# A hybrid attention layer: row sums of full attention from ScalarE's accumulator, V's two parts in one matmul, and another split of PSUM banks in neighbourhood attention

## The chip, the cores and the metric

One Trainium2 chip, one core of it. The metric is the device time of one execution in microseconds (us); lower is better. A core has TensorE (PE in the profile; its weight loads are listed apart as PEld), VectorE (DVE), ScalarE (ACT), GpSimd (POOL) and SyncE (SP, which here issues DMAs). Each engine works through its own list of instructions in order.

## The reference

One encoder layer over 1024 tokens of width 1024, in float32, with a token grid of 16 rows and 64 columns. One input projection feeds two groups of heads:

```python
h = _rmsnorm(x, norm_gain[l]);  proj = h @ w_in[l]
q_a, k_a, v_a, g_a, q_b, k_b, v_b, g_b = jnp.split(proj, split_at, axis=-1)
# group A: 8 query heads, 2 key/value heads, head_dim 64, RMS-normed q/k, axial rope, full attention
sc = jnp.einsum('bqkgd,bskd->bkgqs', qi, k).astype(jnp.float32) * scale
p = jax.nn.softmax(sc, axis=-1)
o_a = jnp.einsum('bkgqs,bskd->bqkgd', p, v) * jax.nn.silu(g_a)
# group B: 8 heads, each query sees a clamped window of 8 rows x 16 columns, with a learned bias
o_b = _neighbourhood_attn(q_b, k_b, v_b, na_rpb[l]) * jax.nn.silu(g_b)
x = x + jnp.concatenate([o_a, o_b], axis=-1) @ w_out[l]
return _rmsnorm(x, final_norm_gain)
```

## The kernel before

Matmuls run on 16-bit operands with float32 precision kept by splitting: a float32 value is a high float16 part plus a low float16 remainder, and a product is hi*hi + hi*lo + lo*hi, so three matmuls stand where one would.

**Stages.** A head of some 85 us normalises x and makes the first weights. Then comes *stage A*, full attention: 64 steps, one for each of 2 key/value heads, 8 blocks of 128 queries and 4 query heads (`run_units(64, ...)`). Then *stage B*, neighbourhood attention: 32 steps, one for each block of 128 queries and pair of heads. Then a tail with the rest of the output projection and the final norm. Here a step of stage A or B is named by its index, from 0.

**A step of stage A.** `a_qk`: four matmuls of 512 columns give 128 x 1024 scores in the PSUM tile `s` (two such tiles take turns); DVE reads them (L732) for the row's shift `nm`; ACT takes the exponential into `p32` (L734) and copies it to the high part (L735). One step later `a_lo` on DVE makes the low part (L740), and a transposing DMA turns both into `pt`. Five steps later `a_pv` multiplies `pt` with V. V stands in `va` as 64 high columns, a column of ones, and 64 low columns. For each of 8 key blocks there are three matmuls: `pt` high by V's high part and the ones (65 columns, L757), `pt` high by V's low part (64 columns, L758), `pt` low by V's high part and the ones (65 columns, L759). Both V parts are added up in the same 64 columns of the PSUM bank `pv`, and the 65th column is the row sum. After four heads `evac` on DVE takes the reciprocal of the sums (L763), scales it (L764) and multiplies (L766).

**A step of stage B.** `b_lo` of the step before (DVE, L845), then `b_qk`: matmuls into two score banks `sb` (L815, L818); for each of two heads DVE adds the bias and takes the minimum (L836), ACT the exponential (L838); ACT copies the high part (L840). Three steps later `b_pv`. The steps of B are written so that DVE has L845, then two L836, then its other work of the step; ACT has some of its other work, then two L838 and L840, then the rest.

**Fill and jobs.** Between the attention matmuls PE is given chunks of projection matmuls (`Flow.fill`, recorded at L494): so many chunks in a step, by `FILL_A`, `FILL_B`. Their results are emptied from PSUM by *jobs* on ACT and DVE (`Flow.job`, `Flow.work`): each step has a budget for ACT and DVE, which is the step's assumed length less what attention itself takes. `BASE_A` and `BASE_B` hold these three numbers (step without fill, ACT's share, DVE's share), and what does not fit the budget waits for a later step. The jobs that prepare weights are: four sums of squares on ACT (L362), a power on POOL (L381), four high parts on ACT (L404), four low parts on DVE (L409). `need_w` issues what is still missing when a matmul asks for a weight. The first 6 steps of A are ordered by a scheduler; all later ones stand as written.

**PSUM banks in stage B.** `bank` hands out four banks, of which the scores use three in turn (`k % 3`); `proj_tile` gives the fourth to the projections, which so have three.

Of the kernel before, what the change touches and what calls it, by code (L numbers as in the profile page):

```python
# [11 lines left out]
AF = mybir.ActivationFunctionType  # L12
OP = mybir.AluOpType
AX = mybir.AxisListType
PSUM = bass.MemoryType.PSUM

P = 128
KC = 8
NU = 8
GC = 256  # L20
NH = 8
D = 64
NX = 4
BASE_A, BASE_B = (1.8, 2.6, 2.9), (1.7, 1.6, 2.0)
HAND = 6
SKEW_A, SKEW_B = 5, 3
FILL_A = [(4, 5.0), (7, 4.2)]
# [20 lines left out]
class Flow:  # L48
# [13 lines left out]
    def at(self, delay, pos, fn, *a):  # L62
        self.due.setdefault((self.slot + delay, pos), []).append((fn, a))

    def job(self, eng, cost, fn, *a, delay=1, late=1, key=None):

        self.jobs.append((late, self.slot + delay, self.number(), eng, cost, fn, a, key))
# [75 lines left out]
def kernel(ctx: ExitStack, tc: tile.TileContext, x: bass.AP, w: bass.AP, wo: bass.AP,  # L143
# [3 lines left out]
    act, dve, pool, pe, sp = nc.scalar, nc.vector, nc.gpsimd, nc.tensor, nc.sync  # L147
# [100 lines left out]
    GX, GXI, GQ, GK, SCA = 51, 52, 53, 54, 55  # L248
# [4 lines left out]
    def col(i, n=1):  # L253
        return sm[:, i:i + n]
# [63 lines left out]
    banks, own = [], []  # L318

    def proj_tile(name):  # L320
        if not banks:
            return ps_p.tile([P, 2, GC], F32, tag="pj", name=name)
        if not own:
            own.extend(ps_p.tile([P, 2, GC], F32, tag="pj", name=f"pjb{i}") for i in range(2))
            own.append(banks[3].rearrange("p (a b) -> p a b", b=GC))
        k = turn["own"] = turn.get("own", -1) + 1
        return own[k % 3]

    spare = [ps_v.tile([P, 512], F32, tag="pv", name=f"pv{i}") for i in range(2)][::-1]

# [188 lines left out]
    kTa = r6(0, [P, NU, 3, P], F16, "kTa")  # L519
    va_all = r6(1, [P, 3072], F16, "va")  # L520
    va_more = va_all[:, 2080:2592].bitcast(BF16)
    va = va_all[:, :NU * 2 * (2 * D + 2)].rearrange("p (u h d) -> p u h d", u=NU, h=2)
    v_hi, v_lo = slice(0, D + 1), slice(D + 2, 2 * D + 2)
    pool.memset(va[:, :, :, D:D + 1], 1.0)
    qTa = [carve(rq, 8192 * i, [NU, 4, P], F16) for i in range(2)]
    klo1 = carve(rq, 16384, [NU, P], F16)

# [56 lines left out]
    def kva_gen(up):  # L584
        def evac(pt):
            both = slot("stg1", [P, 8, P], F16)
            stg, stg_l = both[:, :6].rearrange("p (i a) b -> p i a b", a=3), both[:, 6:]
            vs = pt[:, :, P:].rearrange("p a (h d) -> p a h d", d=D)
            at(1, "pre", lambda: act.activation(va[:, 2 * up:2 * up + 2, :, :D], vs, AF.Copy, scale=2.0 ** -14))

            def vlo():
                for i in range(2):
                    dve.scalar_tensor_tensor(va[:, 2 * up + i, :, v_lo], vs[:, i], 2.0 ** -14,
                                             va[:, 2 * up + i, :, :D], op0=OP.mult, op1=OP.subtract)
            at(1, "mid", vlo)

            def fin(k):
                def hi():
                    act.activation(stg[:, :, :2, :D], k, AF.Copy)
                    act.activation(stg[:, :, :2, D:], k, AF.Copy)  # L600
                at(2, "pre", hi)

                def lo():
                    for h, to in ((0, stg[:, :, 2]), (1, stg_l)):
                        dve.tensor_tensor(to.rearrange("p i (e d) -> p i e d", d=D),
                                          k[:, :, h, None, :].to_broadcast([P, 2, 2, D]),
                                          stg[:, :, h].rearrange("p i (e d) -> p i e d", d=D), op=OP.subtract)
                at(2, "mid", lo)

                def tr():  # L610
                    sp.dma_start_transpose(kTa[:, 2 * up:2 * up + 2].rearrange("p i a t -> p (i a) t"),
                                           both[:, :6].rearrange("p a b -> p (a b)"))
                    sp.dma_start_transpose(klo1[:, 2 * up:2 * up + 2], stg_l.rearrange("p a b -> p (a b)"))
                at(2, "post", tr)
            norm_rope(KVA, up, pt[:, :, :P], 2, 1, fin)
        yield from proj_pair(KVA, up, from_h, evac)
# [100 lines left out]


    pv, sums, pts, hls = {}, {}, {}, {}

    def a_qk(i, hh, u, h):
        s = ps_s.tile([P, 1024], F32, tag="s", name=f"s{hh}_{u}_{h}")
        q = qTa[hh][:, u, h]
        for c in range(2):
            pe.matmul(s[:, c * 512:(c + 1) * 512], q, kTa[:, 4 * c:4 * c + 4, hh], start=True, stop=False)  # L725
        for c in range(2):
            pe.matmul(s[:, c * 512:(c + 1) * 512], q, klo1[:, 4 * c:4 * c + 4] if hh else kTa[:, 4 * c:4 * c + 4, 2],  # L727
                      start=False, stop=True)
        nm = tn(f"nm{hh}_{u}_{h}")
        o = 4096 * (i % RING)  # L730
        hl, p32 = carve(ar, o, [2, 1024], F16), carve(ar, o + 2048, [1024], F32)
        dve.tensor_tensor_reduce(out=hl[:, 1].bitcast(BF16), in0=s, in1=col(SHA).to_broadcast([P, 1024]), scale=col(NSA),  # L732
                                 scalar=3e38, op0=OP.add, op1=OP.min, accum_out=nm)
        act.activation(p32, s, AF.Exp, bias=nm, scale=col(SCA))  # L734
        at(0, "mid", lambda: act.activation(hl[:, 0], p32, AF.Copy))  # L735
        hls[hh, u, h] = (hl, p32)

# [10 lines left out]
    def a_pv(i, hh, u, h):  # L748
        if h == 0:
            if hh + u:  # L750
                spare[:] = [ps_v.tile([P, 512], F32, tag="pv", name=f"pv{hh}_{u}"), spare[0]]
            pv[hh, u] = spare[0][:, :4 * (D + 1)].rearrange("p (h d) -> p h d", h=4)
        late["head"] = h
        o = pv[hh, u][:, h]
        pt = pts.pop((hh, u, h))
        for kt in range(8):
            pe.matmul(o, pt[:, kt], va[:, kt, hh, v_hi], start=kt == 0, stop=False)  # L757
            pe.matmul(o[:, :D], pt[:, kt], va[:, kt, hh, v_lo], start=False, stop=False)  # L758
            pe.matmul(o, pt[:, 8 + kt], va[:, kt, hh, v_hi], start=False, stop=kt == 7)  # L759
        if h == 3:  # L760
            def evac():
                sm4 = tn(f"sum{hh}_{u}", 4, "sum")
                dve.reciprocal(sm4, pv[hh, u][:, :, D])  # L763
                dve.tensor_scalar(sm4, sm4, col(RC + KVA), 2.0 ** 14, op0=OP.mult, op1=OP.mult)  # L764
                m = mixA[u // 2][:, u % 2, hh * GC:(hh + 1) * GC].rearrange("p (h d) -> p h d", d=D)
                dve.tensor_tensor(m, pv[hh, u][:, :, :D], sm4[:, :, None].to_broadcast([P, 4, D]), op=OP.mult)  # L766
# [28 lines left out]
    def bank(kind):  # L795

        if not banks:
            scores.close()
            ps_b = ctx.enter_context(tc.tile_pool(name="ps_b", bufs=1, space=PSUM))
            banks.extend(ps_b.tile([P, 512], F32, tag=f"b{i}", name=f"sb{i}") for i in range(4))  # L800
            banks.extend(ps_v.tile([P, 512], F32, tag="pv", name=f"pvb{i}") for i in range(2))
        k = turn[kind] = turn.get(kind, -1) + 1
        return banks[k % 3 if kind == "sb" else 4 + k % 2]

    sbs = {}

# [239 lines left out]
    k, q = [kva_gen(up) for up in UP], group(1, [qa_gen(0, up) for up in UP])  # L1046
# [132 lines left out]
    a, b = ORDER[2:4]  # L1179
# [25 lines left out]
    with run_units(32, SKEW_B, parts_b, rates(FILL_B, FILL_B_END), hooks2):  # L1205
        pass
    fl.base, fl.early, fl.budget = None, None, {}
    fl.step(0)
    os_start(ORDER[7])
    while fl.queue:  # L1210
# [88 lines left out]
```

## Time and profile before

| | |
|---|---|
| device time, 3 runs | 564.04, 567.51, 570.62 us; median 567.51 us |
| the profiled execution | 566.36 us; its span from first to last instruction is 564.5 us |
| mean granted TensorE clock | 0.977 |
| busy share of the span | PE 91%, PEld 71%, DVE 79%, ACT 65%, POOL 28% |
| stage A | about 85 to 366 us of the span |
| stage B | about 366 to 506 us |
| tail | about 506 to 564.5 us |

In the rows of the profile, "line engine operation out<-in" names an instruction by its line in the kernel; "xN" is a count. A busy PE is not a PE at its peak: consecutive matmuls overlap, so the pace of matmuls is read from the starts of successive ones. A row of the waits reads "engine, tile, line <- what it waited for: us in total, times, longest".

### The profile page before, as it was taken

The page shows a single profiled execution, that of the slowest core. Times are in us where ns is not written, and L with a number is a line of the kernel's source. Part 1 is how long each engine was busy: PE and PEld are TensorE (multiplying, and loading weights), DVE is VectorE, ACT ScalarE, POOL GpSimd, SP SyncE. Part 2 cuts the span into 40 slices and gives each one's busy share as a digit, 9 for nine tenths or more (in the row PEclk, how much of TensorE's full clock was granted, in tenths as well). Part 3 has the DMA queues.
Part 4 walks back from the last instruction along what each step waited for, and adds up shares of the span by engine and source line. Part 5 has one row for each costly group of instructions (what it writes and reads, how often), then busy time and mean ns, then how long its engine had stood idle before and what let it go on. Part 6 is the DMA issues. An engine that isn't in the chain of part 4 may idle for free.

```text
span 564.5 us, 13778 instructions
## 1 busy us (share of the span) xinstructions
PE 515.5 (91%) x5583; PEld 402.4 (71%) x5583; DVE 446.0 (79%) x911; ACT 367.8 (65%) x583; POOL 157.2 (28%) x181
## 2 busy tenths in 40 slices
PE   2577989989999999999999999999998889998994
PEld 0456877767887555568888888887776667788883
DVE  4588788989887988778789887588987798988532
ACT  5546456958787759587696886367777568663211
POOL 2395887670000000000000022433821231224000
PEclk9979999999999999999999999999999998999998
DMA  8999549789999999998999899436586599996612
GB/s 242 220 181 234 122 71 210 125 143 191 203 228 174 175 216 193 193 187 173 211 197 180 189 165 214 129 68 132 105 188 105 117 255 230 181 154 139 215 38 75
DMA packets 244513, 95.47 MB, mean 169 GB/s; under 512 B 235489, under 2 KB 236001, under 8 KB 242530
## 3 DMA queue, kind: packets, MB, share of 16 engines
q1 hardware_dynamic: 240850, 73.89, 71.8%
q0 software_dynamic: 3312, 19.92, 12.2%
q8 instruction: 43, 0.70, 0.5%
q10 hardware_dynamic: 288, 0.79, 0.5%
q14 instruction: 20, 0.16, 0.1%
HBM read 29.56 MB, written 4.19 MB: 60 GB/s over the span
## 4 chain that ended last, share of the span: by engine, by line
PE 51%; DVE 9%; ACT 8%; issue 5%; DMA 4%; SPq 0%; POOL 0%; DVEq 0%; POOLq 0%; ACTq 0%
PE pj L494 19%; PE kb L494 7%; PE pjb L494 5%; PE s L725 4%; PE s L727 4%; ACT rq L838 3%; PE sb L494 3%; PE pv L758 3%; DMA ar<-ar 3%; PE pv L759 3%; PE pv L757 3%; ACT ar L840 3%; DVE ar L836 2%; DVE ar L845 2%; DMA x2b<-in_x_dram 1%
## 5 line engine op out<-in xcount | busy, mean ns | idle before, releaser
L494 PEld LDWEIGHTS <-hT 128*128 128x128 f16 x2112 | 204.9, 100 | 58.8 <-issue 16.2
L494 PE MATMUL pj<-whl,hT 128*128 128x256 f16 x1680 | 201.6, 278 | 20.9 <-DMA hT<-ar 7.8
L734 ACT ACTIVATE ar<-s,nm,sm 128x1024 f32<-128x1024 f32 x64 | 76.9, 1202 | 56.6 <-DVE nm L732 56.3
L732 DVE CUSTOM_DVE_ANT_0 ar<-s,sm 128x1024 bf16<-128x1024 f32 x64 | 82.0, 1281 | 33.9 <-PE s L727 33.6
L494 PEld LDWEIGHTS <-ar 128*128 128x128 f16 x768 | 74.6, 99 | 11.7 <-issue 2.6
L740 DVE TENSOR_TENSOR ar<-ar 128x1024 f16<-128x1024 f32 x64 | 79.5, 1242 | 1.4 <-ACT ar L735 1.4
L735 ACT ACTIVATE ar<-ar 128x1024 f16<-128x1024 f32 x64 | 67.6, 1057 | 2.1 <-DVE sum L764 0.3
L838 ACT ACTIVATE rq<-ar,nm 128x384 f32<-128x384 f32 (+1 forms) x64 | 34.1, 580 | 38.4 <-DVE nm L836 37.7
L494 PE MATMUL pjb<-whl,ar 128*128 128x256 f16 x408 | 47.4, 273 | 0.0
L494 PE MATMUL kb<-hT,whl 128*128 128x512 f16 x192 | 44.5, 379 | 0.0
L409 DVE SCALAR_TENSOR_TENSOR whl<-raw,sm,whl 128x512 f16<-128x512 f32 x52 | 38.7, 770 | 2.8 <-ACT whl L404 2.8
L758 PE MATMUL pv<-va,ar 128*128 128x64 f16 x384 | 40.1, 194 | 0.0
L757 PE MATMUL pv<-va,ar 128*128 128x65 f16 x384 | 40.1, 193 | 0.0
L759 PE MATMUL pv<-va,ar 128*128 128x65 f16 x384 | 39.9, 192 | 0.0
L757 PEld LDWEIGHTS <-ar 128*128 128x128 f16 x384 | 35.7, 97 | 5.5 <-issue 0.3
L758 PEld LDWEIGHTS <-ar 128*128 128x128 f16 x384 | 35.5, 97 | 5.5 <-issue 0.3
L725 PE MATMUL s<-kTa,rq 128*128 128x512 f16 x128 | 38.5, 383 | 0.4 <-ACT ar L734 0.4
L212 POOL DMA_DIRECT2D raw<-in_w_dram x11 | 6.7, 607 | 113.0 <-ACT ar L735 89.0
L845 DVE SCALAR_TENSOR_TENSOR ar<-rq,ar 128x768 f16<-128x768 f32 (+1 forms) x32 | 30.7, 959 | 7.9 <-ACT ar L840 7.5
L879 POOL TENSOR_TENSOR ar<-ar,qkg 128x256 f32<-128x256 f32 x16 | 18.5, 1157 | 65.0 <-DVE qkg L877 63.7
L759 PEld LDWEIGHTS <-ar 128*128 128x128 f16 x384 | 35.5, 99 | 0.0
L404 ACT ACTIVATE whl<-raw,sm 128x512 f16<-128x512 f32 x52 | 34.0, 709 | 1.4 <-POOL sm L381 1.4
(174 smaller groups left out, 978.4 us busy)
## 6 DMA issues: line engine op xcount, KB each, us to landing
raw<-in_w_dram POOLq DMA_DIRECT2D x11, 1024.0 KB, 7.7
raw<-in_wo_dram POOLq DMA_DIRECT2D x4, 1024.0 KB, 6.3
ar<-in_x_dram SPq DMA_DIRECT2D x7, 512.0 KB, 6.3
khh<-ar SPq DMA_DIRECT2D x16, 128.0 KB, 3.4
x2b<-in_x_dram POOLq DMA_DIRECT2D x4, 512.0 KB, 6.9
x<-in_x_dram POOLq DMA_DIRECT2D x4, 512.0 KB, 6.2
out_dram<-x2b SPq DMA_DIRECT2D x8, 256.0 KB, 4.2
out_dram<-x SPq DMA_DIRECT2D x7, 256.0 KB, 2.9
```

Of the source, the lines that this page charges most:

```text
L409: dve.scalar_tensor_tensor(wp[g][1][:, q], raw[g][:, q], col(S_ + g), wp[g][0][:, q], op0=OP.mult, op1=OP.subtract)
L494: pe.matmul(*o[0], **o[1])
L725: pe.matmul(s[:, c * 512:(c + 1) * 512], q, kTa[:, 4 * c:4 * c + 4, hh], start=True, stop=False)
L732: dve.tensor_tensor_reduce(out=hl[:, 1].bitcast(BF16), in0=s, in1=col(SHA).to_broadcast([P, 1024]), scale=col(NSA), scalar=3e38, op0=OP.ad ...
L734: act.activation(p32, s, AF.Exp, bias=nm, scale=col(SCA))
L735: at(0, "mid", lambda: act.activation(hl[:, 0], p32, AF.Copy))
L740: dve.tensor_tensor(hl[:, 1], p32, hl[:, 0], op=OP.subtract)
L757: pe.matmul(o, pt[:, kt], va[:, kt, hh, v_hi], start=kt == 0, stop=False)
L758: pe.matmul(o[:, :D], pt[:, kt], va[:, kt, hh, v_lo], start=False, stop=False)
L759: pe.matmul(o, pt[:, 8 + kt], va[:, kt, hh, v_hi], start=False, stop=kt == 7)
L838: act.activation(p32[:, e], t[:, e], AF.Exp, bias=nm, scale=-1.0)
L845: dve.scalar_tensor_tensor(hl[:, 1], p32, 2.0 ** 14, hl[:, 0], op0=OP.mult, op1=OP.subtract)
```

## The change

- Full attention's row sums no longer come from a column of ones. The exponential on ACT (L734) gets an accumulator output, which adds up its row into a column of a small tile `rsum`; ACT reads this accumulator out after each of the 64 exponentials. The ones in `va` are gone, and so is POOL's memset of them.
- V's high and low parts stand beside each other, 128 columns. `pt` high is multiplied with both in one matmul of 128 columns, `pt` low with the high part in one of 64 columns: two matmuls for three. `pv` now is a full bank of 4 heads x 128 columns.
- `evac` takes the reciprocal of `rsum`, adds the two halves of `pv` with a reduction on DVE (512 elements to 256), and POOL multiplies the result with the scaled reciprocals.
- `BASE_A` goes from (1.8, 2.6, 2.9) to (1.72, 2.8, 2.9): a step is taken as 0.08 us shorter and ACT's share as 0.2 us longer.
- In stage B the scores use four banks in turn, the projections two, until B is over (`late["tail"]`), when the fourth bank is given to the projections as a third.

```diff
-BASE_A, BASE_B = (1.8, 2.6, 2.9), (1.7, 1.6, 2.0)
+BASE_A, BASE_B = (1.72, 2.8, 2.9), (1.7, 1.6, 2.0)
...
-            own.append(banks[3].rearrange("p (a b) -> p a b", b=GC))
-        k = turn["own"] = turn.get("own", -1) + 1
-        return own[k % 3]
+        if "tail" in late and len(own) < 3:
+            own.insert(0, banks[3].rearrange("p (a b) -> p a b", b=GC))
+        own.append(own.pop(0))
+        return own[-1]
...
-    va = va_all[:, :NU * 2 * (2 * D + 2)].rearrange("p (u h d) -> p u h d", u=NU, h=2)
+    va = va_all[:, :NU * 4 * D].rearrange("p (u h d) -> p u h d", u=NU, h=2)
-    pool.memset(va[:, :, :, D:D + 1], 1.0)
...
-        act.activation(p32, s, AF.Exp, bias=nm, scale=col(SCA))
+        if h == 0:
+            rsum[hh, u] = tn(f"sum{hh}_{u}", 4, "sum")
+        act.activation(p32, s, AF.Exp, bias=nm, scale=col(SCA), accum_out=rsum[hh, u][:, h:h + 1])
...
-            pe.matmul(o, pt[:, kt], va[:, kt, hh, v_hi], start=kt == 0, stop=False)
-            pe.matmul(o[:, :D], pt[:, kt], va[:, kt, hh, v_lo], start=False, stop=False)
-            pe.matmul(o, pt[:, 8 + kt], va[:, kt, hh, v_hi], start=False, stop=kt == 7)
+            pe.matmul(o, pt[:, kt], va[:, kt, hh], start=kt == 0, stop=False)
+            pe.matmul(o[:, :D], pt[:, 8 + kt], va[:, kt, hh, :D], start=False, stop=kt == 7)
         if h == 3:
             def evac():
-                sm4 = tn(f"sum{hh}_{u}", 4, "sum")
-                dve.reciprocal(sm4, pv[hh, u][:, :, D])
+                sm4 = rsum.pop((hh, u))
+                dve.reciprocal(sm4, sm4)
                 dve.tensor_scalar(sm4, sm4, col(RC + KVA), 2.0 ** 14, op0=OP.mult, op1=OP.mult)
...
-                dve.tensor_tensor(m, pv[hh, u][:, :, :D], sm4[:, :, None].to_broadcast([P, 4, D]), op=OP.mult)
+                dve.tensor_reduce(out=m, in_=pv[hh, u].rearrange("p h (a d) -> p h d a", a=2), axis=AX.X, op=OP.add)
+                pool.tensor_tensor(m, m, sm4[:, :, None].to_broadcast([P, 4, D]), op=OP.mult)
...
-        return banks[k % 3 if kind == "sb" else 4 + k % 2]
+        return banks[k % 4 if kind == "sb" else 4 + k % 2]
```

The lines of the changed kernel are 1 to 3 higher than those of before: L734 is L737 there, L836 is L839, L838 is L841, L840 is L843, L845 is L848, L915 is L918; L362, L404 and L409 are each one higher.

**TensorE, the start of one `a_pv`** (stage A; `s` are the scores ahead of it, `pv` the bank it fills, a row with LDWEIGHTS loads one block of `pt`). Before, the last score matmul and the first key block:

```order
L727 LDWEIGHTS rq
L727 MATMUL s_1_1_1135<-kTa,rq 128x512
L757 LDWEIGHTS ar
L757 MATMUL pv_102<-va,ar 128x65
L758 LDWEIGHTS ar
L758 MATMUL pv_102<-va,ar 128x64
L759 LDWEIGHTS ar
L759 MATMUL pv_102<-va,ar 128x65
```

After:

```order
L728 LDWEIGHTS rq
L728 MATMUL s_1_1_1136<-kTa,rq 128x512
L760 LDWEIGHTS ar
L760 MATMUL pv_102<-va,ar 128x128
L761 LDWEIGHTS ar
L761 MATMUL pv_102<-va,ar 128x64
```

One load and one matmul of each three pairs are gone, and the first matmul has 128 columns. Of PE's other rows, the small matmuls for some weights' scales (L378) stand one or more steps later.

**ScalarE, stage B, from the copy of step 14 to the tanh behind step 15** (`nm_6`, `nm_7` are step 15's; L915 and L918 are the high parts of the mixed rows, L694 the tanh of a gate; `rest` and `wss` belong to the squares of a weight). Before:

```order
L840 ACTIVATE ar<-rq 128x768
L362 ACTIVATE rest_5101,wss_0_5670<-raw_5668 128x512
L362 ACTIVATE rest_5101,wss_1_5671<-raw_5668 128x512
L362 ACTIVATE rest_5101,wss_2_5672<-raw_5668 128x512
L915 ACTIVATE mhl_5887<-ar,os_5886 128x512 x2
L838 ACTIVATE rq<-ar,nm_6_6008 128x384
L838 ACTIVATE rq<-ar,nm_7_6011 128x384
L840 ACTIVATE ar<-rq 128x768
L694 ACTIVATE ar<-pjb_5196,sm 128x512
```

After:

```order
L843 ACTIVATE ar<-rq 128x768
L918 ACTIVATE mhl_5382<-ar,os_5381 128x512 x2
L841 ACTIVATE rq<-ar,nm_6_5508 128x384
L841 ACTIVATE rq<-ar,nm_7_5511 128x384
L843 ACTIVATE ar<-rq 128x768
L694 ACTIVATE ar<-pjb_4699,sm 128x512
```

Three squares are gone from in front of step 15; the fourth, in front of step 17, is gone from there too, and these four now stand behind steps 18 and 19.

**VectorE, stage B, step 28** (the names `sb` are step 28's scores, `whl` the low parts of the last weight, `rw_16` the factor of the projection with it). Before:

```order
L836 ISA ar,nm_0_6910<-sb_5113,ar,sm 128x384
L836 ISA nm_0_6910 128x1
L836 ISA ar,nm_1_6913<-sb_5111,ar,sm 128x384
L836 ISA nm_1_6913 128x1
L907 ISA rest_5102,os_6859<-ar,os_6859 128x512
L907 ISA os_6859 128x1
L909 TENSOR_SCALAR os_6859<-os_6859 128x1
L409 SCALAR_TENSOR_TENSOR whl_6301<-raw_6273,sm,whl_6301 128x512
L426 RECIPROCAL sm<-sm 128x1
L988 TENSOR_TENSOR rw_16_6935<-os_5624,sm 128x1
L845 SCALAR_TENSOR_TENSOR ar<-rq,ar 128x768
```

After:

```order
L381 TENSOR_SCALAR wss_0_5908<-sb_4602 128x1
L839 ISA ar,nm_0_6406<-sb_4601,ar,sm 128x384
L839 ISA nm_0_6406 128x1
L839 ISA ar,nm_1_6409<-sb_4602,ar,sm 128x384
L839 ISA nm_1_6409 128x1
L910 ISA rest_4592,os_6349<-ar,os_6349 128x512
L910 ISA os_6349 128x1
L912 TENSOR_SCALAR os_6349<-os_6349 128x1
L410 SCALAR_TENSOR_TENSOR whl_5926<-raw_5906,sm,whl_5926 128x512 x4
L427 RECIPROCAL sm<-sm 128x1
L991 TENSOR_TENSOR rw_16_6428<-os_5125,sm 128x1
L848 SCALAR_TENSOR_TENSOR ar<-rq,ar 128x768
```

The last weight's scale (L381), its four high parts on ScalarE and its four low parts (L410) now all belong to step 28; before, the scale belonged to step 25 and three of the low parts to step 26.

More of the change, by code (lines that the diff above doesn't have):

```diff
@@ L592, in vlo @@
                 for i in range(2):
-                    dve.scalar_tensor_tensor(va[:, 2 * up + i, :, v_lo], vs[:, i], 2.0 ** -14,
+                    dve.scalar_tensor_tensor(va[:, 2 * up + i, :, D:], vs[:, i], 2.0 ** -14,
                                              va[:, 2 * up + i, :, :D], op0=OP.mult, op1=OP.subtract)
@@ L719 @@
     pv, sums, pts, hls = {}, {}, {}, {}
+    rsum = {}
     def a_qk(i, hh, u, h):
@@ L751, in a_pv @@
                 spare[:] = [ps_v.tile([P, 512], F32, tag="pv", name=f"pv{hh}_{u}"), spare[0]]
-            pv[hh, u] = spare[0][:, :4 * (D + 1)].rearrange("p (h d) -> p h d", h=4)
+            pv[hh, u] = spare[0].rearrange("p (h d) -> p h d", h=4)
         late["head"] = h
@@ L1207 @@
     fl.base, fl.early, fl.budget = None, None, {}
+    late["tail"] = True
     fl.step(0)
```

## The prediction

> **What bounds the kernel now.** I read the busy time by stage first, then what each engine waited for within a stage, then single rows. In the first fence each row is a stretch of the span and the busy time of PE, PEld, DVE, ACT and POOL in it, then the granted clock; behind it stand waits, first of 136 to 360 us, then of 366 to 506 us.
>
> ```profile
> 136.00:360.00 224.00, 224.00 (x2665) 166.45 (x2663) 185.14 (x318) 170.00 (x224) 18.23 (x31) 1.00 1.00 190
> 366.00:506.00 140.00, 129.03 (x1432) 102.31 (x1430) 118.71 (x305) 99.93 (x189) 44.28 (x48) 0.98 0.79 153
> 506.00:548.00 42.00, 40.58 (x411) 36.31 (x410) 26.02 (x76) 12.30 (x31) 8.89 (x12) 1.00 0.61 145
> ...
> DVE ar L732 <- PE s L727: 33.3, 40, 1.8
> ACT ar L734 <- DVE nm L732: 48.6, 38, 2.5
> ...
> DVE ar L845 <- ACT ar L840: 7.5, 11, 1.5
> DVE ar L699 <- ACT ar L694: 6.6, 2, 3.6
> PE sb L815 <- DVE nm L836: 9.1, 6, 2.7
> ```
>
> Stage A is bound by PE: in 224 us PE is never idle, at full clock, while DVE waits 33.3 us for PE's scores and ACT 48.6 us for DVE. Time that PE saves there is saved; up to 33 us more on DVE and 48 us more on ACT have room, if they are spread. Stage B is another matter. No wait of DVE for scores is among its waits; PE waits 9.1 us for DVE to free score banks, and DVE, busy 118.71 of 140 us, waits for ACT. So B goes by the loop of DVE and ACT, and PE runs ahead until the banks stop it. In the tail PE is busy 40.58 of 42 us; its work there is not changed, and it gets its third bank back.
>
> **Stage A: what PE saves.** The first two rows are runs of projection matmuls from the chain, with 256 and 512 columns; behind them the first and the last of the 24 matmuls of one `a_pv`, and what follows.
>
> ```profile
> 154.36 2.62 PE pj L494 x24
> 182.65 2.59 PE kb L494 x12
> ...
> 202.05 0.19 PE L757 MATMUL pv<-va,ar 128*128 128x65 f16 x1
> 202.75 0.19 PE L759 MATMUL pv<-va,ar 128*128 128x65 f16 x1
> 202.78 2.10 PE L494 MATMUL kb<-hT,whl 128*128 128x512 f16 x9
> ...
> L757 PEld LDWEIGHTS <-ar 128*128 128x128 f16 x384 | 35.7, 97 | 5.5 <-issue 0.3
> ```
>
> The paces are 2.62/24 = 109.2 ns for 256 columns, 2.59/12 = 215.8 ns for 512, and (202.78 - 202.05)/24 = 30.4 ns for 64 or 65. Each of these matmuls has a load of its own of some 97 ns, and none of the paces shows it, so loads lie under the matmuls. A matmul of 128 columns does not occur before. Its bounds are its neighbours, 30.4 and 109.2 ns; I take the line through 256 and 512 columns, 0.4164 ns a column, which gives 109.2 - 128 x 0.4164 = 55.9 ns (it gives 29.2 for 64, close to the 30.4 measured). A key block then costs 55.9 + 30.4 = 86.3 ns for 3 x 30.4 = 91.2 ns: 4.9 ns saved, and 8 blocks x 64 heads = 512 of them make **2.5 us**. The bounds make it between 15.6 us saved and 24.8 us lost.
>
> The Trainium skill speaks against this: TensorE: Matmul & The Clock Gate, section "Back-to-back issue gap", puts a sustained stream of pairs of load and matmul at about 81 ns each for 128 columns and 131 ns for 512. By it the block would cost 81 + 30.4 = 111.4 ns, and the 512 blocks an estimated 10.3 us more than now. The trace's 215.8 ns for 512 columns does not agree with it.
>
> **Stage A: what the other engines get.**
>
> ```profile
> L362 ACT ACTIVATION_READ_ACCUMULATOR va<-raw 128x1 f32 x36 | 6.8, 188 | 0.0
> L545 DVE TENSOR_REDUCE nt<-ar 128x8 f32<-128x512 f32 x4 | 2.7, 680 | 1.9 <-ACT ar L542 1.9
> L766 DVE TENSOR_TENSOR ar<-pv,sum 128x256 f32<-128x256 f32 x16 | 6.8, 425 | 0.6
> L879 POOL TENSOR_TENSOR ar<-ar,qkg 128x256 f32<-128x256 f32 x16 | 18.5, 1157 | 65.0 <-DVE qkg L877 63.7
> ```
>
> ACT: 64 reads of the accumulator at 188 ns, 12.0 us, under its 48.6 us of waiting; the exponential's result is needed by PE five steps later. DVE: a reduction of 512 elements (680 ns, another shape; its bounds are L766's 425 ns and twice that) for a product of 425 ns, 16 x 0.255 = 4.1 us, under its 33.3 us; uncovered, 4.1 us would be the price. POOL: 16 products of some 1157 ns, 18.5 us on an engine that was busy 18.23 of 224 us; the gate that reads them comes some steps later. DVE and ACT budgets shrink by 0.08 and 0.28 us a step, so weights are ready later, which costs A nothing while PE does not ask for them early. The six steps under the scheduler, up to some 125 us, have DVE's normalisation in another order, with the same instructions; I cost them at 0, between 1.5 us better and worse.
>
> **Stage B: what the moved jobs do.** The order moves squares, high and low parts of the weights by one to three steps. Step 15 is the clearest place.
>
> ```profile
> 424.56 0.61 ACT L362 ACTIVATE rest<-raw 128x512 bf16<-128x512 f32 x1
> 424.64 0.55 POOL L910 TENSOR_TENSOR os<-os,mh 128x1 f32<-128x1 f32 x1 [2.02 <-DVE os L909]
> 426.26 0.08 DVE L836 DVE_READ_ACCUMULATOR2_ANT nm<- 128x1 f32 x1
> 426.68 1.32 ACT L915 ACTIVATE mhl<-ar,os 128x512 f16<-128x512 f32 x2
> 427.91 1.11 ACT L838 ACTIVATE rq<-ar,nm 128x384 f32<-128x384 f32 x2
> 429.80 0.67 ACT L694 ACTIVATE ar<-pjb,sm 128x512 f32<-128x512 f32 x1
> 430.50 0.69 DVE L699 SCALAR_TENSOR_TENSOR ar<-ar,pjb 128x512 f32<-128x512 f32 x1 [3.62 <-ACT ar L694]
> ...
> 438.48 0.61 ACT L362 ACTIVATE rest<-raw 128x512 bf16<-128x512 f32 x1
> 439.09 1.32 ACT L915 ACTIVATE mhl<-ar,os 128x512 f16<-128x512 f32 x2
> 442.91 0.69 DVE L699 SCALAR_TENSOR_TENSOR ar<-ar,pjb 128x512 f32<-128x512 f32 x1 [2.97 <-ACT ar L694]
> ```
>
> DVE stands idle for 3.62 us, since the gate's tanh (L694) comes behind step 15's exponentials, and these behind three squares. Without the squares the two L915 could start when POOL has their scale, at 425.19, and end at 426.51 for 428.00; the exponentials then start at 426.51, since their `nm` is there at 426.34. That is 1.4 us, and DVE's next wait is for the same tanh. Step 17 loses one square: 439.09 - 438.48 = 0.6 us.
>
> ```profile
> 379.26 0.61 ACT L362 ACTIVATE rest<-raw 128x512 bf16<-128x512 f32 x1
> 381.81 0.90 ACT L838 ACTIVATE rq<-ar,nm 128x256 f32<-128x256 f32 x2
> 384.01 1.41 DVE L409 SCALAR_TENSOR_TENSOR whl<-raw,sm,whl 128x512 f16<-128x512 f32 x2 [1.25 <-ACT whl L404]
> ...
> 379.39 0.69 DVE L845 SCALAR_TENSOR_TENSOR ar<-rq,ar 128x512 f16<-128x512 f32 x1 [1.24 <-ACT ar L840]
> 486.95 0.75 DVE L409 SCALAR_TENSOR_TENSOR whl<-raw,sm,whl 128x512 f16<-128x512 f32 x1 [0.87 <-ACT whl L404]
> ```
>
> In step 4 two squares go from in front of the exponentials; ACT had 1.4 us of them there and could start 1.1 us earlier, and DVE's 1.25 us wait for L404 shrinks as much. Together 1.4 + 0.6 + 1.1 = 3.1 us gained. Against it: behind step 19 ACT now has three squares and L902, 4 x 0.8 us, some 0.6 us more than DVE has to do meanwhile. Step 26 loses its three low parts, and a step where DVE has no other work leaves it idle for some 1.2 us, as at 379.39; the 0.87 us wait at 486.95 goes with them, so 0.3 us lost. Step 28 gets all of the last weight: after the second `nm` DVE has 1.0 us of L907 and L909, but ACT still has an exponential, the copy (1.3 us in all) and the first high part (0.7): 1.1 us idle, and PE's last chunk, `b_pv` and scores behind the last low part cost DVE some 0.6 us more. Lost: 0.6 + 0.3 + 1.7 = 2.6 us. So B gains **0.5 us**, a difference of terms that I give 3.5 us each way.
>
> The banks I cost at 0: no wait of DVE for scores is in the list, so a fourth score bank lets PE run further ahead of an engine that sets the pace. Two banks for projections are enough while a tile takes 8 chunks, nearly two steps at 4.2 chunks, and is emptied one step after it is full; PE waits there instead, and if it waits too long, the 9.1 us of cover is what is used up first. Bounds: 9.1 us gained, and some 3 us lost, if PE stood one of its longest waits (2.7 us) without cover.
>
> **The sum.** 566.36 (the profiled execution, its span and 1.9 us around it) - 2.5 - 0.5 = 563.4 us. This execution lies 1.15 us below the median of the three runs, 567.51, whose spread is 6.6 us; I give **563.5 us**, 0.7% under that median. 1% (561.8 and 573.2 us) is about what a measurement of this kernel can tell from no change.
>
> **The rivals.** *The fourth bank pays.* PE's stops would cost time in B, because PE's clock falls after one and its fill is late for the gates. For it: the waits of 9.1 us vanish. Against it: DVE does not wait for PE. It gives 563.4 - 9.1 = 554.3 us.
>
> *The banks or the moved weights cost.* The last weight is made in the step that needs it, and projections with two banks wait for DVE. For it: step 28's rows. B then loses 2.6 us and a bank's 3 us without the gains: 566.4 - 2.5 + 5.6 = 569.5 us. The change in A, too, could come to nothing, if a 128-column matmul took 60.8 ns, twice 30.4; that is 566 us, between this case and mine.
>
> *POOL's product stops DVE* (slower). A running POOL product held DVE's L575 to 1.75 us, and PE then waited for DVE:
>
> ```profile
> 121.97 2.13 POOL L559 TENSOR_TENSOR ar<-ar 128x512 f32<-128x512 f32 x1
> 122.90 1.75 DVE L575 TENSOR_TENSOR ar<-ar 128x512 f16<-128x512 f32 x1
> 125.59 1.44 PE L494 MATMUL pj<-whl,hT 128*128 128x256 f16 x6 [2.72 <-DVE wss L380]
> ...
> L732 DVE CUSTOM_DVE_ANT_0 ar<-s,sm x64: 1265/1283/1286, 87.2 to 347.4; 128x1024 bf16<-128x1024 f32 x64
> ```
>
> Sixteen products of 1.16 us follow `evac`. If every third brought such a wait, 5 x 2.72 = 13.6 us would be lost: 577 us. It decides from the point where DVE's step, longer by 1.16 + 0.26 us, leaves no slack of its 33.3 us / 40 waits = 0.8 us and the lag grows over the following steps. Against it: in 11 of 16 places the next DVE instruction is L732, which reads scores from PSUM, lasts longer than the product, and never took over 1286 ns, although POOL worked beside it at times. The Trainium skill (SBUF — State Buffer, "Who interferes with whom") says that a DVE instruction with two SBUF inputs contends with a POOL instruction that reads SBUF, one with a single SBUF input does not; L575 agrees with the first half.
>
> *A 128-column matmul with its load partly bare* (slower). For it: the load's row of 97 ns is longer than the matmul. Midway between its bounds, at 82.5 ns, a block costs 112.9 ns, 512 x 21.7 = 11.1 us more than now: 577 us. It decides above 60.8 ns. Against it: 30.4 ns with the same load. The Trainium skill's page on TensorE, named above, has 81 ns for this pace.
>
> **How the numbers follow.** My case, 560 to 567 us: 0.57. The fourth bank pays: 0.18. Banks or weights cost, or A's gain comes to nothing: 0.16. POOL: 0.06. The bare load: 0.03. A third of my case lies under 561.8 us, so faster by over 1%: 0.19 + 0.18 and some of the scheduler's steps, 0.39; within 1%: 0.52; slower: 0.09. The range reaches from the fourth bank's case to the one where banks or weights cost: 554 to 570 us.
>
> **What would show it.** In A: a pace of 55 to 57 ns behind each 128-column matmul, an `a_pv` of 0.69 us for 0.73, PE still without idle time, ACT's accumulator reads at 188 ns, DVE waiting less than 33 us for scores. In B: no long wait of L699 at step 15 but one of some 2.2 us, and waits at steps 26 and 28; PE's waits at score banks gone or small, without B being shorter by as much. I am wrong if PE idles in A, if the 128-column pace is over 60 ns, or if B's length moves by more than 4 us.

## The result, and the profile after

The changed kernel took 569.92 us (median of 20 runs, 567.72 to 577.45); the kernel before, run beside it, 569.42 us (20 runs). The ratio is **1.0046 [1.0024, 1.0067]**, so the change makes the kernel 0.5% slower, some 2.6 us. A second set of 12 runs (e1 below) gave 1.0072 [1.0030, 1.0115]. The forecast was 0.7% faster.

The rows here come from the changed kernel's second profiled execution (575.29 us, span 573.5), because its first fell into a disturbed run. That is 3.7 us above the median of its set, while the profiled execution of the kernel before (566.36 us) lies 2 to 3 us below the medians of its sets, so a length read from them is weighed below against the runs. The busy times by stage, shifted to where the stages now lie (B ends 8 us later), columns as in the prediction:

```profile
134.00:358.00 224.00, 224.00 (x2246) 166.22 (x2244) 189.71 (x325) 176.52 (x280) 27.98 (x45) 1.00 1.02 192
364.00:514.00 150.00, 128.23 (x1394) 100.07 (x1393) 120.50 (x309) 99.74 (x189) 44.24 (x49) 0.94 0.78 147
514.00:556.00 42.00, 42.00 (x439) 37.88 (x438) 25.81 (x76) 12.08 (x29) 8.32 (x12) 1.00 0.69 145
```

Stage A is as it was: PE without idle time at full clock, and the new work lies on ACT (170.00 to 176.52), POOL (18.23 to 27.98) and DVE (185.14 to 189.71). Stage B is the one that changed. Its stretch is 10 us longer, while DVE's busy time grew by 1.8 us only, and PE's granted clock fell from 0.98 to 0.94. The waits, first of 136 to 360 us, then of 366 to 520 us:

```profile
ACT ar L737 <- DVE nm L733: 41.1, 44, 2.6
DVE ar L733 <- PE s L728: 27.1, 31, 1.7
...
DVE ar L848 <- ACT ar L843: 8.8, 12, 1.5
DVE ar L839 <- DMA ar<-ar: 7.8, 2, 4.7
PE pjb L495 <- ACT whl L405: 7.3, 1, 7.3
PE pvb L868 <- DMA ar<-ar: 6.5, 2, 5.6
DVE ar L699 <- ACT ar L694: 5.1, 2, 2.9
PE sb L818 <- DVE nm L839: 0.2, 1, 0.2
```

DVE and ACT still wait in A, less than before (27.1 for 33.3 us, 41.1 for 48.6), as work that fits under PE should make it. In B the 9.1 us of PE's waits for score banks are gone. Two new ones stand in their place: PE waits 7.3 us, once, for the high parts of a weight, and 6.5 us for transposing DMAs. Not all of the 10 us is the change's doing: 7.8 us are two waits of DVE for such DMAs (4.7 and 3.1 us), which e11 below, with the same order of jobs, has at 0.7 us at most; they are taken up under "What stays open".

**Where the first of them is.** It is step 28. These are the kernel before, DVE's two score reads at the start of steps 28 and 29 with the one low part between them, and PE:

```profile
492.18 0.61 DVE L836 CUSTOM_DVE_ANT_0 ar<-sb,ar,sm 128x384 f32<-128x384 f32 x1
494.11 0.74 DVE L409 SCALAR_TENSOR_TENSOR whl<-raw,sm,whl 128x512 f16<-128x512 f32 x1
495.91 0.61 DVE L836 CUSTOM_DVE_ANT_0 ar<-sb,ar,sm 128x384 f32<-128x384 f32 x1
...
491.07 1.47 PE L494 MATMUL sb<-whl,ar 128*128 128x256 f16 x12
492.38 0.19 PE L865 MATMUL pvb<-rq,ar 128*128 128x65 f16 x1
```

And the changed kernel, DVE, ACT and PE at the same place, with three stretches of the windows view behind them (PE's busy time first, the granted clock third from the end):

```profile
495.43 0.62 DVE L839 CUSTOM_DVE_ANT_0 ar<-sb,ar,sm 128x384 f32<-128x384 f32 x1 [3.13 <-DMA ar<-ar]
498.05 2.54 ACT L405 ACTIVATE whl<-raw,sm 128x512 f16<-128x512 f32 x4
498.81 0.37 PE L495 MATMUL pjb<-whl,ar 128*128 128x256 f16 x1 [7.29 <-ACT whl L405]
498.79 2.74 DVE L410 SCALAR_TENSOR_TENSOR whl<-raw,sm,whl 128x512 f16<-128x512 f32 x4 [1.34 <-ACT whl L405]
499.60 2.50 PE L495 MATMUL pjb<-whl,ar 128*128 128x256 f16 x11 [0.42 <-DVE whl L410]
501.89 0.26 PE L868 MATMUL pvb<-rq,ar 128*128 128x65 f16 x1
504.19 0.62 DVE L839 CUSTOM_DVE_ANT_0 ar<-sb,ar,sm 128x384 f32<-128x384 f32 x1 [1.53 <-PE sb L821]
...
491.00:498.80 7.80, 0.51 (x5) 0.31 (x4) 3.29 (x11) 3.47 (x8) 2.52 (x3) 0.76 1.06 206
498.80:503.70 4.90, 4.48 (x34) 2.86 (x33) 3.83 (x7) 3.02 (x5) 0.00 (x0) 0.50 0.01 3
503.70:506.00 2.30, 2.30 (x16) 1.56 (x16) 1.81 (x6) 1.09 (x2) 0.00 (x0) 0.66 0.79 149
```

From one step's first score read to the next it was 495.91 - 492.18 = 3.73 us, and is 504.19 - 495.43 = 8.76 us: 5.03 us more in one step. DVE stands idle for 1.34 us until ACT has made the first high part. It makes four low parts (2.74 us) where it made one (0.74). Then it waits 1.53 us for step 29's scores, since PE comes late: having stood 7.29 us, PE runs at a granted clock of 0.50, and its matmuls of 256 columns take (501.89 - 499.60)/11 = 208 ns each, for (492.38 - 491.07)/12 = 109 ns before. 1.34 + 2.00 + 1.53 = 4.87 of the 5.03 us. How much of the 1.53 us is the clock's is read from these rows; no run has the late weight without the half clock.

The Trainium skill has a rule for this clock: TensorE: Matmul & The Clock Gate, section "What's actually happening", says that an idle window of about 3.4 us puts the array to half its clock, and that it takes about as long a busy stretch to get it back. The trace agrees on the half clock behind a stop of this length. The way back took longer here: the clock is 0.50 for 4.90 us, in which PE is busy 4.48 us, and still 0.66 in the mean of the next 2.30 us.

### The profile page after: what moved, and what is told of

It is laid out like the page before. It is cut to its first block, busy times and chain, and to the rows that moved or that the text cites. A ratio compares the mean times of both kernels' runs of the same rounds, so it can differ in the third digit from the quotient of the medians.

```text
span 575.7 us, 12845 instructions
## 1 busy us (share of the span) xinstructions
PE 515.3 (90%) x5071; PEld 400.0 (69%) x5071; DVE 449.1 (78%) x911; ACT 373.9 (65%) x647; POOL 166.4 (29%) x196
## 4 chain that ended last, share of the span: by engine, by line
PE 50%; DVE 9%; DMA 8%; ACT 7%; issue 4%; POOL 0%; DVEq 0%; POOLq 0%; ACTq 0%
PE pj L495 17%; PE pjb L495 8%; DMA ar<-ar 8%; PE kb L495 6%; PE pv L760 4%; PE s L726 4%; PE s L728 4%; ACT rq L841 3%; PE pv L761 2%; ACT ar L843 2%; PE sb L495 2%; DVE ar L848 2%; DVE ar L839 2%; DVE whl L410 1%; ACT rest L363 1%
## 5 line engine op out<-in xcount | busy, mean ns | idle before, releaser
L737 ACT ACTIVATE ar<-s,nm,sm 128x1024 f32<-128x1024 f32 x64 | 76.9, 1202 | 53.3 <-DVE nm L733 40.5
L495 PEld LDWEIGHTS <-ar 128*128 128x128 f16 x768 | 75.4, 100 | 19.8 <-issue 10.0
L495 PE MATMUL pjb<-whl,ar 128*128 128x256 f16 x480 | 59.6, 282 | 6.0 <-ACT whl L405 3.1
L841 ACT ACTIVATE rq<-ar,nm 128x384 f32<-128x384 f32 (+1 forms) x64 | 34.1, 580 | 45.0 <-DVE nm L839 44.3
L495 PE MATMUL pjb<-whl,hT 128*128 128x256 f16 x432 | 50.6, 273 | 0.9 <-DVE ar L699 0.8
L495 PE MATMUL kb<-hT,whl 128*128 128x512 f16 x192 | 46.2, 390 | 0.0
L769 POOL TENSOR_TENSOR ar<-ar,sum 128x256 f32<-128x256 f32 x16 | 11.0, 686 | 116.5 <-DVE ar L768 112.3
L760 PE MATMUL pv<-va,ar 128*128 128x128 f16 x384 | 39.7, 221 | 5.0 <-DMA ar<-ar 5.0
L760 PEld LDWEIGHTS <-ar 128*128 128x128 f16 x384 | 34.3, 99 | 10.7 <-DMA ar<-ar 5.5
L410 DVE SCALAR_TENSOR_TENSOR whl<-raw,sm,whl 128x512 f16<-128x512 f32 x52 | 38.7, 772 | 2.0 <-ACT whl L405 2.0
L761 PE MATMUL pv<-va,ar 128*128 128x64 f16 x384 | 38.4, 194 | 0.0
L848 DVE SCALAR_TENSOR_TENSOR ar<-rq,ar 128x768 f16<-128x768 f32 (+1 forms) x32 | 30.4, 950 | 9.0 <-ACT ar L843 8.8
L761 PEld LDWEIGHTS <-ar 128*128 128x128 f16 x384 | 33.6, 99 | 5.2
L495 PEld LDWEIGHTS <-whl 128*128 128x128 f16 x192 | 18.0, 101 | 19.5 <-issue 2.2
```

What stands on the lines that cost most here:

```text
L410: dve.scalar_tensor_tensor(wp[g][1][:, q], raw[g][:, q], col(S_ + g), wp[g][0][:, q], op0=OP.mult, op1=OP.subtract)
L495: pe.matmul(*o[0], **o[1])
L737: act.activation(p32, s, AF.Exp, bias=nm, scale=col(SCA), accum_out=rsum[hh, u][:, h:h + 1])
L760: pe.matmul(o, pt[:, kt], va[:, kt, hh], start=kt == 0, stop=False)
L761: pe.matmul(o[:, :D], pt[:, 8 + kt], va[:, kt, hh, :D], start=False, stop=kt == 7)
L841: act.activation(p32[:, e], t[:, e], AF.Exp, bias=nm, scale=-1.0)
```

## The experiments

The ratios are against the kernel before in the same set of runs (medians 568.3, 568.5 and 568.7 us), each experiment with 12 runs. The last column is the ratio applied to that median, not the difference of the two medians.

| | what | median us | ratio [95%] | us against before |
|---|---|---|---|---|
| e1 | the changed kernel again | 571.56 | 1.0072 [1.0030, 1.0115] | +4.1 |
| e2 | full attention's part alone | 564.76 | 0.9957 [0.9923, 0.9991] | -2.4 |
| e3 | the banks alone | 567.53 | 1.0001 [0.9967, 1.0036] | +0.1 |
| e4 | the two numbers of `BASE_A` alone | 572.59 | 1.0095 [1.0062, 1.0127] | +5.4 |
| e5 | e2 and e3 together | 566.72 | 0.9963 [0.9934, 0.9991] | -2.1 |
| e6 | changed, low parts early | 565.92 | 0.9958 [0.9931, 0.9985] | -2.4 |
| e7 | ACT's number alone | 568.88 | 1.0002 [0.9975, 1.0028] | +0.1 |
| e8 | before, last weight late | 572.71 | 1.0079 [1.0046, 1.0111] | +4.5 |
| e9 | e4, low parts early | 568.03 | 1.0006 [0.9972, 1.0040] | +0.3 |
| e10 | e2, low parts early | 567.17 | 0.9965 [0.9935, 0.9994] | -2.0 |
| e11 | e2 and e4 together | 572.44 | 1.0052 [1.0017, 1.0087] | +3.0 |

**The change in its three parts: e1 to e4.** e1 is the changed kernel as it stands.

> The changed kernel again, for a trace beside those of its parts. All theories: between 0.2 and 0.7% slower than before (1 to 4 us), as measured. The theories differ in where the trace shows it. Theory 1, the banks: stage A, from its first score matmul to B's first, is 2 to 3 us shorter than before's 281.0 us, and stage B with its tail is 4 to 6 us longer, with PE waiting at projection tiles. Theory 2, the new work of stage A (accumulator read, longer evac, POOL's product) or its transposes: stage A is not shorter, and PE idles there, where before it did not. Theory 3, the budgets: stage A is shorter, B is longer at steps 19 to 29, where weights come late, and no bank is waited for.

e2 takes the changed kernel and puts two parts back:

```diff
-BASE_A, BASE_B = (1.72, 2.8, 2.9), (1.7, 1.6, 2.0)
+BASE_A, BASE_B = (1.8, 2.6, 2.9), (1.7, 1.6, 2.0)
...
-        return banks[k % 4 if kind == "sb" else 4 + k % 2]
+        return banks[k % 3 if kind == "sb" else 4 + k % 2]
```

with `proj_tile` as before.

> The change in full attention alone: accumulator sums, V's parts in one matmul, evac with POOL's product; BASE_A and the banks as before. Theory 1: 2.5 us faster than before (ratio 0.9955). Theory 2: 1 to 4 us slower than before, as slow as the whole change. Theory 3: 2.5 us faster, as theory 1.

e3 is the kernel before with the new `bank` and `proj_tile`:

> The banks of stage B alone: four for scores, two for projections, the third back in the tail; full attention and BASE_A as before. Theory 1: 4 to 6 us slower than before (ratio 1.007 to 1.011). Theories 2 and 3: within 1 us of before.

e4 is the kernel before with one line changed:

```diff
-BASE_A, BASE_B = (1.8, 2.6, 2.9), (1.7, 1.6, 2.0)
+BASE_A, BASE_B = (1.72, 2.8, 2.9), (1.7, 1.6, 2.0)
```

> BASE_A alone, (1.72, 2.8, 2.9) in place of (1.8, 2.6, 2.9): only jobs on ACT and DVE move, no work is added. Theory 3: 4 to 6 us slower than before, lost in stage B. Theories 1 and 2: within 1 us of before.

Full attention's part gains 2.4 us, the banks do nothing that can be measured, and one line with two numbers loses 5.4 us. The sum, +3.1 us, lies between the two measurements of the whole, +2.6 and +4.1 us. So the loss is not in what the change adds but in the jobs that the two numbers move.

**Do they add up: e5 and e11.** e5 is the changed kernel with the old `BASE_A`, e11 the changed kernel with the old banks.

> The changed kernel with BASE_A as before: full attention and banks new, budgets old. The squares and parts of the weights stand in stage B as before. Both theories of the loss (the last weight made in the step that needs it; or the many other jobs that moved) say 2 to 3 us faster than before, as the change in full attention alone (ratio 0.995 to 0.997). If banks and full attention together cost something that neither does alone, it is slower than that.

> The changed kernel with the old split of banks: the full-attention part and the new numbers of BASE_A. My theory (the two effects add, and the banks do nothing): 568.4 x (0.996 + 0.0088) = 571 us, ratio 1.002 to 1.008, with PE waiting some 4 us or more for the last weight's high parts, and no wait of PE of 4 to 5 us for a transposing DMA near 460 us. Rival (the banks make the late weight worse, or the wait at the transposing DMA near 460 us that the profiles with four score banks show is a real cost of the banks): 566 to 568 us, ratio 0.996 to 1.000.

Both come out as the sum of their parts: 0.9963 for 0.9957 + 0.0001, and 1.0052 for 0.9957 + 0.0095. e11's step 28, with three score banks and no long wait for a transposing DMA ahead of it (0.20 us for 3.13), DVE first, then PE, then the windows view:

```profile
490.48 0.62 DVE L838 CUSTOM_DVE_ANT_0 ar<-sb,ar,sm 128x384 f32<-128x384 f32 x1 [0.20 <-DMA ar<-ar]
493.84 2.74 DVE L409 SCALAR_TENSOR_TENSOR whl<-raw,sm,whl 128x512 f16<-128x512 f32 x4 [1.33 <-ACT whl L404]
499.25 0.62 DVE L838 CUSTOM_DVE_ANT_0 ar<-sb,ar,sm 128x384 f32<-128x384 f32 x1 [1.53 <-PE sb L820]
...
493.86 0.37 PE L494 MATMUL sb<-whl,ar 128*128 128x256 f16 x1 [4.28 <-ACT whl L404]
...
493.80:499.20 5.40, 4.92 (x35) 2.98 (x35) 3.84 (x7) 3.07 (x6) 0.00 (x0) 0.50 0.01 3
```

The step is 499.25 - 490.48 = 8.77 us long, as in the changed kernel (8.76), though PE stood 4.28 us and not 7.29: what DVE loses does not hang on how long PE waited, but on the late weight and on the slow PE after it.

**One of the two numbers: e7.** The kernel before with ACT's number alone, `BASE_A = (1.8, 2.8, 2.9)`:

> The kernel before with ACT's number in BASE_A alone raised from 2.6 to 2.8: some jobs of stage A move, the last weights of stage B stand as before. Theory late weight: within 1 us of before. Theory other jobs: 2 to 4 us slower, some of the 5.4 us that both numbers together cost.

Ratio 1.0002: 0.2 us less budget for ACT alone costs nothing. The step number alone was not run.

**The late weight made by hand: e8.** The kernel before, with nothing moved but the last weight (number 16), whose squares are held back by three steps:

```diff
-            squares(g, 4)
+            squares(g, 7 if g == 16 else 4)
```

> The kernel before, BASE_A as before, with one thing changed: the squares of the last weight come three steps later, so that its scale, its four high parts and its four low parts all fall into step 28 of stage B, as in the changed kernel. Theory late weight: 4 to 6 us slower than before (ratio 1.007 to 1.010), lost between the scores of steps 28 and 31, with PE waiting 4 to 7 us for the weight's high part. Theory other jobs: within 1.5 us of before, since a step's worth of moved work has room.

It costs 4.5 us. Its step 28, PE and DVE:

```profile
496.78 0.37 PE L494 MATMUL sb<-whl,ar 128*128 128x256 f16 x1 [4.62 <-ACT whl L404]
...
493.42 0.60 DVE L836 CUSTOM_DVE_ANT_0 ar<-sb,ar,sm 128x384 f32<-128x384 f32 x1
496.76 2.74 DVE L409 SCALAR_TENSOR_TENSOR whl<-raw,sm,whl 128x512 f16<-128x512 f32 x4 [1.33 <-ACT whl L404]
502.06 0.62 DVE L836 CUSTOM_DVE_ANT_0 ar<-sb,ar,sm 128x384 f32<-128x384 f32 x1 [1.42 <-PE sb L818]
...
496.70:501.60 4.90, 4.41 (x32) 2.86 (x31) 3.84 (x7) 3.09 (x6) 0.00 (x0) 0.50 0.02 5
```

The same two waits, 1.33 and 1.42 us, the same half clock, and a step of 8.64 us. From the first score read of step 26 to that of step 29 it took 16.60 us (485.46 to 502.06) for 12.31 before (483.60 to 495.91), 4.3 us more: as far as one profile shows it, the runs' 4.5 us lie there.

**The late weight taken away: e6 and e9.** A weight's raw values are loaded one step after the last low part of the weight two before it (`if g + 2 < 17: at(1, "pre", load_w, g + 2)`, in `lo`), so a low part that a budget puts off delays every second weight behind it, the last one in the end. e6 is the changed kernel with the low parts of the weights 13 and 14 issued without regard to the budget:

```diff
-            job("dve", 1.0 if "b" in late else 0.72, lo, i, delay=0, late=0.5 if g > 11 else 2, key=g)
+            job("dve", 1.0 if "b" in late else 0.72, lo, i, delay=0, late=0 if g in (13, 14) else 0.5 if g > 11 else 2, key=g)
```

> The changed kernel with its new BASE_A, but the low parts of the weights 13 and 14 aren't held back by DVE's budget (late=0 for them). All else of the moved jobs stays moved, but the last weight is ready one to two steps before step 28. Theory late weight: 4 to 5 us faster than the changed kernel, ratio to before 0.995 to 0.998, and no wait of PE for the last weight's high part (7.3 us in the changed kernel's trace). Theory other jobs: as slow as the changed kernel, 1.004 to 1.007.

The last weight's squares then stand in front of step 22 and its high parts in front of step 26. The ratio goes from 1.0046 and 1.0072 to 0.9958, with all else of the change in place. Step 28 of e6, DVE, then PE:

```profile
490.09 0.60 DVE L839 CUSTOM_DVE_ANT_0 ar<-sb,ar,sm 128x384 f32<-128x384 f32 x1
492.01 0.74 DVE L410 SCALAR_TENSOR_TENSOR whl<-raw,sm,whl 128x512 f16<-128x512 f32 x1
493.81 0.61 DVE L839 CUSTOM_DVE_ANT_0 ar<-sb,ar,sm 128x384 f32<-128x384 f32 x1
...
492.81 2.67 PE L495 MATMUL pjb<-whl,ar 128*128 128x256 f16 x23 [1.11 <-DVE whl L410]
```

3.72 us, as before the change. e9 does the same to e4, so that what is left are the moved jobs alone, without full attention's part, the banks or a late weight:

> Before, with the two new numbers of BASE_A and with the low parts of the weights 13 and 14 issued without regard to the budget, so that no weight is late. What is left of the change is the moved jobs alone: squares gone from in front of steps 3, 4 and 15. My theory (the loss is the last weight in step 28, and the other moved jobs are worth what the prediction said, a little under 3 us): 565.5 us, ratio 0.993 to 0.999. Rival (the moved jobs are worth nothing even where no weight is late, since PE or the DMA queue takes the 1.4 and 1.1 us back): 568.3 us, ratio 0.999 to 1.002. Rival (it is the shrunken budgets in A, not the lateness in B, that cost): over 570.5 us, ratio over 1.004.

The ratio is 1.0006 [0.9972, 1.0040]: my theory's 0.993 to 0.999 would have put it under 1. The estimate lies where the rival has it, that the moved jobs are worth nothing, though the interval does not rule out the upper end of the theory's range. Against e4, the late weight costs 0.0095 - 0.0006 = 0.0089, some 5 us, known to about 2.7 us either way.

**A better version: e10.** e2 with e6's edit, to see whether early low parts are a gain of their own:

> The full-attention part with the old numbers of BASE_A and the old split of banks, and with the low parts of the weights 13 and 14 issued without regard to the budget. If the early low parts are a gain of their own, beside taking away the lateness: below the full-attention part alone, 562 to 564 us, ratio 0.988 to 0.993. If they only take away the lateness (there is none with the old numbers): as the full-attention part alone, 566 us, ratio 0.994 to 0.998.

They are not (0.9965 for e2's 0.9957). Four kernels, e2, e5, e6 and e10, are faster than the kernel before by 0.35 to 0.43%, and so than the changed one, and the runs don't tell them apart. The simplest is e2, the full-attention part with the old numbers.

## Why the prediction was wrong

**Stage A: right.** The start of one `a_pv` in the changed kernel, its end and what follows:

```profile
197.80 0.22 PE L760 MATMUL pv<-va,ar 128*128 128x128 f16 x1
197.86 0.19 PE L761 MATMUL pv<-va,ar 128*128 128x64 f16 x1
...
198.45 0.19 PE L761 MATMUL pv<-va,ar 128*128 128x64 f16 x1
198.48 2.75 PE L495 MATMUL kb<-hT,whl 128*128 128x512 f16 x12
```

198.48 - 197.80 = 0.68 us for 8 key blocks (predicted 0.69), 85 ns a block (86.3). Between 130 and 360 us the next matmul starts 56.6 ns behind one of 128 columns (mean of 466, estimated 55.9) and 28.3 ns behind one of 64. The Trainium skill's 81 ns (TensorE: Matmul & The Clock Gate, "Back-to-back issue gap") does not hold here. From A's score matmuls of step 16 to the start of B the changed kernel took 2.6 us less (206.64 for 209.27), e2 2.0 us; the prediction's 2.5 us for 64 steps are 1.9 us for these 48. e2's runs say 2.4 us (0.5 to 4.4).

```profile
L737 ACT ACTIVATION_READ_ACCUMULATOR ar<-s,nm,sm 128x1 f32 x64 | 12.3, 192 | 0.0
L769 POOL TENSOR_TENSOR ar<-ar,sum 128x256 f32<-128x256 f32 x16 | 11.0, 688 | 110.2 <-DVE ar L768 110.2
L768 DVE TENSOR_REDUCE ar<-pv 128x256 f32<-128x512 f32 x16 | 10.9, 684 | 1.4 <-PE pv L761 1.4
```

ACT's reads (192 ns for the 188 taken) and DVE's reduction (684 for 680) were sized right; POOL's product takes 688 ns, not 1157. All three are hidden. The rivals in which POOL's product stops DVE or the load lies bare are out: from 134 to 358 us PE never stood, and the pace is 56.6 ns.

**The banks: right in the sum, by e3.** PE's 9.1 us of waits were cover, as the prediction held: they are gone, and the time is the same.

**Stage B: wrong, in the step "What the moved jobs do".** It gave 3.1 us gained, 2.6 lost. The loss is sized too small, about half of the gain came, and a term is missing.

*Step 28* was the right place with the right mechanism, sized at 1.7 us. Its first part, 1.1 us of DVE waiting for the first high part, measured 1.33 to 1.34 us. Its second, 0.6 us for PE's work behind the low parts, measured 1.42 to 1.53 us: PE's chunk and the scores were priced at full clock, and came at half. That a stop of PE lowers its clock stood in the prediction, but only as a reason for a gain, in the first rival. The three low parts, 2.0 us, were taken as moved from step 26 and so as free; but step 26 gave back only 1.4 us of them (4.96 us became 3.58 in e4 and e8, with DVE waiting 1.49 us at step 27's L845), 0.6 us lost for the 0.3 predicted. e8 prices step 28 and what step 26 gives back together: 4.5 us (2.6 to 6.3), where the prediction has 1.7 + 0.3.

*The gains* were 1.4 + 0.6 + 1.1 us at steps 15, 17 and 4. One of DVE's waits in step 4 before, then its waits in e4, which has the moved jobs alone, in order of time from step 4 to step 17:

```profile
381.33 0.69 DVE L703 TENSOR_TENSOR ar<-ar,pjb 128x512 f32<-128x512 f32 x1 [0.44 <-ACT ar L694]
...
382.89 1.69 DVE L409 SCALAR_TENSOR_TENSOR whl<-raw,sm,whl 128x512 f16<-128x512 f32 x2 [0.64 <-ACT whl L404]
392.42 0.69 DVE L845 SCALAR_TENSOR_TENSOR ar<-rq,ar 128x512 f16<-128x512 f32 x1 [0.64 <-ACT ar L840]
...
399.40 1.44 DVE L409 SCALAR_TENSOR_TENSOR rest<-raw,sm,rest 128x512 f16<-128x512 f32 x1 [0.93 <-ACT rest L404]
...
429.72 0.69 DVE L699 SCALAR_TENSOR_TENSOR ar<-ar,pjb 128x512 f32<-128x512 f32 x1 [2.27 <-ACT ar L694]
441.52 0.69 DVE L699 SCALAR_TENSOR_TENSOR ar<-ar,pjb 128x512 f32<-128x512 f32 x1 [2.88 <-ACT ar L694]
```

Step 15 did what was said: 3.62 us became 2.27, 1.35 us less for the 1.4. So did step 4: its 1.25 became 0.64, and the wait of 0.44 us is gone, 1.05 us for the 1.1. Step 17's became 2.88 for 2.97, 0.1 us and not 0.6: the tanh comes sooner by the square, but DVE has a low part less ahead of its wait (it makes that one later), and so comes to it sooner too. Against these stand new waits: 0.64 us ahead of step 7's scores, and 0.93 us in step 8, whose low part has to wait for a postponed high part. The prediction followed each job from the place that it left and looked for waits at only some of the places that it came to.

Added up over the rows from step 4 to the start of step 24, DVE is idle for 13.7 us in e4, for 12.9 before. Of these, 2.7 and 0.5 us are waits for transposing DMAs, which differ between executions; without them it is 11.0 for 12.4. e2 and e11 have fewer such waits (0.4 and 1.3 us), and differ in the two numbers alone. From the first score read of step 4 to that of step 24, e2 first, with DVE's busy time third:

```profile
375.37:469.64 94.27, 84.30 (x944) 66.76 (x943) 79.75 (x200) 69.20 (x131) 32.61 (x35) 0.98 0.79 154
380.75:473.79 93.04, 83.82 (x935) 65.92 (x933) 79.70 (x199) 68.39 (x128) 31.41 (x34) 0.96 0.81 157
```

The same work, 1.2 us shorter, where the prediction has 3.1 gained less 0.6 lost at step 19, 2.5 us.

*What was missing:* work that shrunken budgets push out of A. Step 0 of B in e4 has at its end a low part and five small instructions that stood in A before, then step 1's first:

```profile
368.98 0.74 DVE L409 SCALAR_TENSOR_TENSOR whl<-raw,sm,whl 128x512 f16<-128x512 f32 x1
...
370.46 0.17 DVE L488 TENSOR_SCALAR sm<-vf 128x4 f32<-128x4 f32 x1
370.54 0.69 DVE L845 SCALAR_TENSOR_TENSOR ar<-rq,ar 128x512 f16<-128x512 f32 x1
```

370.54 - 368.98 = 1.56 us. In A, where DVE waits for PE, they were free, and their leaving gained nothing (209.27 us from step 16 to B, with them and without); in B, where DVE sets the pace, they are paid: from the first score read of step 0 to that of step 4 e4 took 14.59 us for 12.99 (365.50 to 380.09, 367.01 to 380.00). "Weights are ready later, which costs A nothing" was true, and the bill came in B. The parts add up: from step 0's first score read to step 31's, e11's profile is 4.5 us longer than e2's (142.39 for 137.91), 1.6 us in steps 0 to 3, 1.2 us less in 4 to 23, 4.1 us in 24 to 28 and nothing behind. The prediction has 0, 2.5 less and 2.0. The runs of e4 have 5.4 us (3.5 to 7.2).

**The rival that came out.** The case "the banks or the moved weights cost" was given 569.5 us and, together with A's gain coming to nothing, a chance of 0.16. Its half on the weights is what happened, its half on the banks is not: e3 is level. That its 569.5 us is close to the 569.92 measured is luck: it counts 3 us for banks that cost nothing and 2.6 us for weights that cost about twice as much.

**What stays open.** In the profiles of e1, e3 and e5, which have four score banks, PE stands 4.4 to 5.6 us in front of a `b_pv` between 456 and 471 us, and DVE behind it; in e3:

```profile
PE pvb L866 <- DMA ar<-ar: 7.8, 4, 5.1
DVE ar L837 <- DMA ar<-ar: 5.0, 2, 3.8
```

e2, e4 and e11, with three, show no wait of PE for that DMA over 2 us, but e7 and e8, with three, show one of 2.8 and one of 3.4 us there, and e6, with four, none over 1.4 us. e3's profiled execution was 3.5 us above the median of its runs and e5's 2.4 us, so this wait may be in some executions and not in others, or a gain of the banks may hide it; its cause wasn't tried. Nor was that of DVE's 3.13 us in front of step 28, which e1 alone has. Nor is it settled why A's first 16 steps, the scheduled ones among them, are 0.1 to 4.3 us shorter than before in the profiles of e1, e2, e4, e6 and e9 to e11. Some of it is the execution's own: e2 and e5 have the same stage A and took 67.51 and 71.18 us for these steps.

## What to carry to other kernels

A budget that shrinks where an engine has room does not save the work, it sends it on to the next stage; ask what the engine is worth there, and which matmul asks for the last piece. Where a moved job lets TensorE stand for as long as here (3.8 us and more), price the work behind the stop at half the clock, and count the waits at the place where the job arrives as well as at the one that it leaves. When parts of a change can be switched one by one, a tuning number that came with them deserves its own run: here it took back twice what the rest had gained.

## What the runs showed of the hardware

After stops of 3.8 to 7.3 us in step 28, PE's granted clock was 0.50 for the 4.9 to 5.4 us that were read in each of four kernels (e1, e4, e8, e11), whatever the length of the stop. A shorter stop did it in part: in the kernel before, behind the 2.72 us that the prediction shows at 125.59 us, the clock was 0.63 in the mean from 126 to 130 us. So the 1.3 us that DVE waited for the late weight were followed by 1.4 to 1.5 us of waiting for a slow PE one step later, where the estimate had 0.6. The second thing is that 128 columns after a load of 98 ns start every 56.6 ns, the load hidden, though the load is the longer of the two.
